# Moving a 256 MB ifftshift through two DMA queues: sixteen-row steps in sequence, against sixteen-row steps sorted into eight classes

## The chip, the cores and the metric

The kernel runs on one core of one Trainium2 chip. The metric is device time in microseconds (us). The core has 16 DMA engines, and every byte of this kernel is moved by them, from DRAM to DRAM; no compute engine touches the data. Both the input and the output hold 8192 x 8192 numbers of 4 bytes, 268.44 MB each.

## The reference

`reference(x)` is `np.fft.ifftshift(x)` on an 8192 x 8192 float32 array. For even sizes that is a swap of diagonal quadrants: `out[r, c] = x[(r + 4096) % 8192, (c + 4096) % 8192]`. No arithmetic is done on the values. Half a row, 4096 numbers or 16 KB, is the longest run that stays contiguous on both sides.

## The kernel before, in words

The output is written as half rows. The left halves (columns 0 to 4095) go through the queue of SyncE (SP, `nc.sync`), the right halves through the queue of ScalarE (ACT, `nc.scalar`). Neither engine does anything but issue DMAs. A helper, `copy` (line 26), works out the source address (line 28) and issues one DMA (line 29) whose source and destination have the same dimensions.

A **step** in this document is 16 neighbouring output rows in one half. It is 16 packets of 16 KB, one for each of the 16 DMA engines: the outermost dimension, `[C, ENGINES]`, has one row for each engine. The rows of a step lie 32 KB apart, so a step spans 512 KB of the array. There are 512 steps in each half; number them from the top of the output, so that step n holds rows 16n to 16n + 15, and consecutive steps lie 512 KB apart. The source of step n is step n + 256 (modulo 512) of the input, in the other half.

A DMA (`back`, line 45) moves 16 steps in falling order: each engine's next packet lies 16 rows, 512 KB, ahead of the last. That is a block of 256 rows and 4096 KB. The loops of lines 47 and 48 go through the 32 blocks from the bottom of the output up, in groups of four. SP takes the blocks of a group in the order 3, 2, 1, 0 (line 49); ACT takes them in the order 1, 0, 3, 2 (line 50). ACT's first block lacks its top step: that step is moved ahead of the loop by seven small DMAs (lines 36 to 42), cut into four strips of 4 KB columns, three of which are cut again by rows (14 + 2, 9 + 7, 4 + 12). So some DMA engines get more small packets than others before the large ones begin, and ACT's sequence has one step less in its first block (`rest`, line 46).

Each DMA gets one of eight completion semaphores in turn. A DMA that takes a semaphore for the second time first waits, on its queue, for the earlier DMA that used it. In the steady part each queue therefore has at most four DMAs in flight.

Of the kernel before, what the change touches and what calls it, by code (L numbers as in the profile page):

```python
# [1 line left out]

# [4 lines left out]


ENGINES = 16


@with_exitstack
def kernel(
    ctx: ExitStack,
    tc: tile.TileContext,
    x: bass.AP,
    out: bass.AP,
):
    nc = tc.nc
    R, C = x.shape  # L20
    hr = R // 2
    hc = C // 2
    per = 16
    rows = ENGINES * per

    def copy(queue, row, col, dims):

        src = (row + hr) % R * C + (col + hc) % C
        queue.dma_start(
            out=bass.AP(out.tensor, out.offset + row * C + col, dims),  # L30
            in_=bass.AP(x.tensor, x.offset + src, dims),
        )

    start = R - 3 * rows
    strip = hc // 4
    for n, k in enumerate((14, 9, 4)):
        col = hc + n * strip
        copy(nc.scalar, start + rows - ENGINES, col, [[C, k], [1, strip]])  # L40
        copy(nc.scalar, start + rows - ENGINES + k, col, [[C, ENGINES - k], [1, strip]])
    copy(nc.scalar, start + rows - ENGINES, hc + 3 * strip, [[C, ENGINES], [1, strip]])


    back = [[C, ENGINES], [-ENGINES * C, per], [1, hc]]
    rest = [[C, ENGINES], [-ENGINES * C, per - 1], [1, hc]]
    for first in range(R - 4 * rows, -1, -4 * rows):
        for n in (3, 2, 1, 0):
            copy(nc.sync, first + n * rows + rows - ENGINES, 0, back)
            right = first + (n + 2) % 4 * rows  # L50
            if right == start:
                copy(nc.scalar, right + rows - 2 * ENGINES, hc, rest)
            else:
                copy(nc.scalar, right + rows - ENGINES, hc, back)


# [1 line left out]
_INS = ['x']  # L58
_OUTS = [((8192, 8192), 'float32')]


# [23 lines left out]
```

## Time and profile before

| what | number |
|---|---|
| time, median of 3 runs | 812.53 us (809.41 to 813.4) |
| profiled execution: span from the first to the last instruction | 810.9 us |
| bytes read and written | 268.44 MB each |
| packets | 17,520, of them 16,368 of 16 KB |
| DMAs issued by SP / ACT | 32 / 39 |

The page of the profile has no work of TensorE, VectorE or ScalarE in it, and 0.2 us of GpSimd. What matters is in its second part (how busy the 16 DMA engines are in 40 slices of the span, and how many GB/s they move), its third part (the two queues: q1 is SP's, q10 is ACT's; their packets and the share of the engines' time that these took) and its sixth (which DMAs were issued, how large). A rate in GB/s counts each byte once, though each is read and written. Besides the page, the trace keeps a record of every packet: its start, its duration, its queue and its size, but not its engine. The profiled span lies inside the range of the three timed runs, 1.6 us under their median, and little lies around it: the first packet starts 2.2 us after the span begins, and the last one ends 1.2 us before it ends.

### The profile page before, as it was taken

The numbers are of one execution on the slowest core, as the hardware profiler recorded it, in microseconds if no ns is written. First come the engines' busy times: TensorE is split into PE (matmuls) and PEld (weight loads), VectorE is DVE, ScalarE is ACT, GpSimd is POOL, SyncE is SP. The second block draws the span as 40 slices with busy tenths as digits, with TensorE's granted clock in tenths as the row PEclk, the third lists the DMA queues.
The fourth block names the chain that finished last, engine by engine and source line by source line (L and its number), as shares of the span: only waits on it lengthen the run. The fifth ranks groups of instructions, "written<-read, shape, count | busy, mean of one in ns | idle before, by whom it ended". The sixth has DMA issues, their size and how long they took to land. (4 is left out here: it accounts for less than half of the span.)

```text
span 810.9 us, 116 instructions
## 1 busy us (share of the span) xinstructions
POOL 0.2 (0%) x4
## 2 busy tenths in 40 slices
POOL 0000000000000000000000000000000000000000
DMA  9999999999999999999999999999999999999998
GB/s 302 328 335 329 334 333 331 331 335 330 326 331 329 331 335 330 332 332 337 335 336 333 333 337 330 334 335 331 336 331 333 335 334 335 333 330 336 333 338 296
DMA packets 17520, 268.44 MB, mean 331 GB/s; under 512 B 1088, under 2 KB 1088, under 8 KB 1152
## 3 DMA queue, kind: packets, MB, share of 16 engines
q1 hardware_dynamic: 8704, 134.22, 49.7%
q10 hardware_dynamic: 8816, 134.22, 49.6%
HBM read 268.44 MB, written 268.44 MB: 662 GB/s over the span
## 5 line engine op out<-in xcount | busy, mean ns | idle before, releaser
L69 POOL MEMSET const-bfloat16-1.0<- 128x1 bf16 x1 | 0.1, 102 | 0.0
L69 POOL MEMSET const-uint8-127<- 128x1 uint8 x1 | 0.1, 102 | 0.0
L69 POOL MEMSET const-float32-0.0<- 128x1 f32 x1 | 0.1, 99 | 0.2 <-issue 0.2
L69 POOL MEMSET const-float32-1.0<- 128x1 f32 x1 | 0.1, 99 | 0.0
## 6 DMA issues: line engine op xcount, KB each, us to landing
out_dram<-in_x_dram SPq DMA_DIRECT2D x32, 4096.0 KB, 100.9
out_dram<-in_x_dram ACTq DMA_DIRECT2D x31, 4096.0 KB
out_dram<-in_x_dram ACTq DMA_DIRECT2D x1, 3840.0 KB
out_dram<-in_x_dram ACTq DMA_DIRECT2D x1, 64.0 KB, 10.8
out_dram<-in_x_dram ACTq DMA_DIRECT2D x1, 56.0 KB
out_dram<-in_x_dram ACTq DMA_DIRECT2D x1, 48.0 KB
out_dram<-in_x_dram ACTq DMA_DIRECT2D x1, 36.0 KB
out_dram<-in_x_dram ACTq DMA_DIRECT2D x1, 28.0 KB
```

The source lines that it names most:

```text
L69: nc = _bacc.Bacc("TRN2", target_bir_lowering=False, num_devices=1)
```

## The change

The steps are sorted into eight **classes**: the class of a step is its number modulo 8, so two steps of one class lie a multiple of 4 MB apart (8 steps of 512 KB). The output is also cut into eight **parts** of 1024 rows (64 steps, 32 MB). A DMA now moves the eight steps of one class in one part, in rising order: each engine's next packet lies 128 rows, 4 MB, further on. That is 2048 KB instead of 4096 KB, so each queue issues 64 DMAs.

The order is set by two loops. `apart` goes from 0 to 7; for each `a` from 0 to 7, `b` is `a ^ apart` (exclusive or). SP moves the left halves of class a in part b, and ACT the right halves of class b in part a. When `apart` is 0 both queues name the same rows; otherwise they name different classes and different parts. Over the loops all 64 pairs of classes occur once. The small strips at the start and the shorter first block of ACT are gone.

```diff
+CLASSES = 8
...
-    per = 16
-    rows = ENGINES * per
+    block = ENGINES * CLASSES
+    steps = R // (block * CLASSES)
 
-    def copy(queue, row, col, dims):
-
+    def copy(queue, cls, part, left):
+        row = part * steps * block + cls * ENGINES
+        col = 0 if left else hc
         src = (row + hr) % R * C + (col + hc) % C
+        dims = [[C, ENGINES], [block * C, steps], [1, hc]]
         queue.dma_start(
...
-    start = R - 3 * rows
-    strip = hc // 4
-    for n, k in enumerate((14, 9, 4)):
-        col = hc + n * strip
-        copy(nc.scalar, start + rows - ENGINES, col, [[C, k], [1, strip]])
-        copy(nc.scalar, start + rows - ENGINES + k, col, [[C, ENGINES - k], [1, strip]])
-    copy(nc.scalar, start + rows - ENGINES, hc + 3 * strip, [[C, ENGINES], [1, strip]])
...
-    back = [[C, ENGINES], [-ENGINES * C, per], [1, hc]]
-    rest = [[C, ENGINES], [-ENGINES * C, per - 1], [1, hc]]
-    for first in range(R - 4 * rows, -1, -4 * rows):
-        for n in (3, 2, 1, 0):
-            copy(nc.sync, first + n * rows + rows - ENGINES, 0, back)
-            right = first + (n + 2) % 4 * rows
-            if right == start:
-                copy(nc.scalar, right + rows - 2 * ENGINES, hc, rest)
-            else:
-                copy(nc.scalar, right + rows - ENGINES, hc, back)
+    for apart in range(CLASSES):
+        for a in range(CLASSES):
+            b = a ^ apart
+            copy(nc.sync, a, b, True)
+            copy(nc.scalar, b, a, False)
```

## The prediction

> **What bounds the kernel now.** I read the second and third part of the page first: how busy the DMA engines are, and with whose packets.
>
> ```profile
> span 810.9 us, 116 instructions
> ...
> DMA  9999999999999999999999999999999999999998
> GB/s 302 328 335 329 334 333 331 331 335 330 326 331 329 331 335 330 332 332 337 335 336 333 333 337 330 334 335 331 336 331 333 335 334 335 333 330 336 333 338 296
> ...
> q1 hardware_dynamic: 8704, 134.22, 49.7%
> q10 hardware_dynamic: 8816, 134.22, 49.6%
> HBM read 268.44 MB, written 268.44 MB: 662 GB/s over the span
> ```
>
> The 16 engines are busy 99.3% of the span (49.7 + 49.6), so nothing waits for an instruction: the end is set by how long packets take. Each engine carries 1,024 packets' worth of 16 KB. The waits of SP's queue confirm that issuing is not the bound:
>
> ```profile
> SPq L29 <- DMA out_dram<-in_x_dram: 686.8, 28, 28.4
> ```
>
> SP stands 686.8 us waiting for an earlier DMA to land before it may issue the next; one issue itself takes 0.57 us in the trace.
>
> So the question is what a packet takes. In the packet records the shortest 16 KB packets take 0.61 us (a third of all, 5,534 of 16,368, lie at or under 0.615), the median 0.73, the mean 0.786, a tenth over 1.07. At 0.611 for all of them the copy would last 1024 x 0.611 = 626 us: some 180 us are packets that are stretched by traffic, and only the addresses and the order of packets can change that. That is what this change does.
>
> **What the trace tells of classes.** An engine's next packet starts 3 to 4 ns before the recorded end of its last one, so the records fall into 16 chains, and counting a queue's packets along a chain gives the step of each. Three readings follow.
>
> (a) All engines keep together: at any time their positions in a queue differ by at most 3 steps, and 93% of an engine's packets alternate between the queues. SP runs 5 to 7 steps ahead of ACT. So the classes of the two queues differ by 1 to 5 at any moment, never by 0.
>
> (b) The class of the step matters. The mean packet of classes 0 to 7 takes 777, 771, 758, 739, 813, 832, 806 and 798 ns. Sorted by the pair (SP's class, ACT's class) the rate of the engines together goes from 320 GB/s for (5, 1) to 358 for (7, 3). But it is no simple function of the difference: mean packets at differences of 1 to 5 are 791, 785, 787, 784 and 790 ns.
>
> (c) Fewer classes in flight cost a little. I take 1 over the sum of squared shares of the classes among the 16 packets in flight as their effective number. It averages 3.5; the mean rate is 333.7. Moments with 4.5 to 5 have 338.5, those under 2.5 (894 moments of 7,474) have 331.5. And while one queue was alone, near the start, all engines were in about 2 classes:
>
> ```profile
> 4.00:23.50 19.50, 0.00 (x0) 1.00 1.00 328
> ```
>
> ```profile
> 18.00:23.50 5.50, 0.00 (x0) 1.00 1.00 319
> ...
> 45.00:805.00 760.00, 0.00 (x0) 1.00 1.00 333
> ```
>
> These are stretches with their GB/s at the end: first nearly all SP and then nearly all ACT, with the strips; then ACT almost alone; then the steady part.
>
> **The change part by part.** I work against the profiled execution: 2.2 us to the first packet, 807.6 us of packets, 1.2 us behind, 810.9 in all.
>
> *Two classes in flight instead of three to five (`apart` 1 to 7, seven eighths of the bytes).* Both queues are issued from 0.73 us on with the same work, so they run within about a step of each other, and a DMA stays in one class for eight steps. The 16 engines are then in class a and class b only. The row for that is reading (c): 331.5 against 333.7. 7/8 x 807.6 = 706.7 us, times 333.7/331.5 - 1 = 0.66%: **+4.7 us**. That all 64 pairs come up adds nothing, since differences of 1 to 5 are alike in (b), and 6 and 7 are 2 and 1 with the queues exchanged. Bounds: if all stages ran like the best pair, 807.6 x 333.7/358 = 753 us, -55; like the worst, 807.6 x 333.7/320 = 842 us, +35.
>
> *One class in flight (`apart` 0, one eighth).* Not in the trace. The nearest row is a queue alone, 319 to 328. I take the slower, 319, since one class is further away than the two there: 100.9 us x (333/319 - 1) = 4.4%: **+4.4 us**. Bounds: the two halves of the same rows, moved one after the other by one engine, could also help; 358 gives -7, and all packets like the class-5 mean (832 against 786 ns) +6.
>
> *Steps 4 MB apart in one queue.* About half of a queue's packets in flight are now one or two steps off in the same class, where before they were one class off. No packets in the trace of before lie so. I take nothing beyond the two terms above, because engines at different steps are in different rows of the 16; below, I take the -55 of the best pair as an end. The upper end is a packet like those over 1 us (2,455 of them, mean 1.155 us): 1024 x 1.155 = 1,183 us. A rule of the Trainium skill speaks against the change here (page "DMA: Bandwidth & Descriptors", section "Latency and other measured facts"): copies between HBM tensors whose rows lie 4 MiB apart ran at 103 GB/s, at 512 KiB apart at 207. An estimate by that page's ratio alone would be 810.9 x 207/103, about 1,630 us. The rule concerns rows moved side by side at that pitch; the trace of before has no such pitch, and side by side the engines stay 32 KB apart here, so no run yet shows it.
>
> *Strips and semaphores.* The seven small DMAs go: 64 packets of 185 ns on 16 engines, **-0.7 us**. DMAs go from 71 to 128, all on 16 engines, so completion packets (4 bytes, 9 ns each) go from 1,088 to 2,048: 960 x 9 / 16 ns = **+0.5 us**.
>
> *Issues.* 57 more, by two queues, at 0.57 to 0.65 us each. They lie beside the packets: when a queue's oldest DMA lands, three more of 8 steps are in flight, 24 packets of an engine at 2 x 0.786 us, 38 us of cover against 0.6 us. Before it was 48 packets. Without this cover each issue would add its 0.6 us plus about 1.4 us to its first packet (the 2.18 us at the start, less the issue's 0.73): 64 x 2 = 128 us. Engines that differ by 3 steps can't use up 24.
>
> *Start and end.* The first 37.8 us after the first packet already run at 334 GB/s, so the simpler start gains nothing. At the end SP's packets stop at 806.0 us and ACT's at 809.7, the 16 engines' last ones within 1.5 us; I count 0, with 1 us to either side. The rising order instead of the falling has no row; 0, inside the bounds of the pairs.
>
> Sum: 4.7 + 4.4 - 0.7 + 0.5 = +8.9 us, 819.8 us on the profiled execution. That one lies 1.6 us under the median of the runs, so **821 us**.
>
> **The rivals.**
>
> *Faster: the new pairs are better ones.* Reading (b) shows pairs from 320 to 358 GB/s, and before covers only 20 of the 64 often. The best six, three with ACT in class 3, one with ACT in class 2 and two with SP in class 3, lie at 340 to 358, in the mean 348.5. If the new pairs are like these, the packets take 807.6 x 333.7/348.5 = 773 us, 777 with start and end. For it: these six lie 2% to 7% over the mean. Against it: in (b) a slow class is slow in either queue (4 to 7 over 0 to 3), and every class has as many packets as before. Half of that gain would be 794.
>
> *No change: only the class's own time counts.* Then the mean of 786 ns stays, whatever the partner, and the single-queue rows are chance (319 is from 5.5 us, some 107 packets). The sum is -0.7 + 0.5: 812 us.
>
> *Much slower: steps of 4 MB collide.* Decides as soon as engines of one queue, a step apart, stand in each other's way. If the 4 packets or so of 16 that are a step off make their kind go at 1.155 us, a quarter of packets is 0.37 us longer, 0.09 us on the mean: 1024 x 0.09 = 94 us, 905 in all; if all do, 1,183. Against it: (a), engines mostly share a step.
>
> *The change doesn't do what it says: the queues drift.* If one gets ahead by 4 steps, half of a DMA's time goes beside the next pair. The classes in flight are then three, and the first term shrinks to some 2 us: 818. That is within the forecast.
>
> **Chances.** What a measurement of this kernel can tell from no change is about 0.5%, 4 us: 808.5 to 816.5 counts as the same. Forecast (two classes in flight, 816.5 to 860): 0.48. Faster pairs, under 808.5: 0.27, of it 0.08 under 785. Same: 0.15. Collisions over 860: 0.10. So faster 0.27, same 0.15, slower 0.58. The range goes from 785 to 860 and leaves out 0.18. The bound of the best pairs (753) and of the collisions (1,183) lie outside it, with those chances; the forecast's own case is 816.5 to 860.
>
> **What would show it.** In the profile after, the 40 slices tell the stages: the first five slices (`apart` 0) should lie at about 319 GB/s and the rest at 330 to 333, with the engines at 99% throughout. If the first eighth is as fast as the rest, the second term is wrong. If all slices lie over 340, the pairs are better ones; if all lie under 310, the 4 MB step costs. Slices in which the engines fall under 95% would mean that queues run dry, which I cost at nothing. A share of packets at 0.61 us that rises with an unchanged mean would say that the stretched ones got longer.

## The result, and the profile after

The changed kernel takes 821.42 us (median of 4 runs, 819.48 to 823.92), the kernel before 811.9 us (809.41 to 813.4) beside it. The ratio is 1.0126, with a 95% interval of 1.0098 to 1.0153: slower, by 9.5 us between the medians. The forecast was 821 us, and its sum +8.9 us.

The page of the changed kernel, second and third part (busy tenths of the DMA engines in 40 slices, GB/s in the same slices, then the queues):

```profile
span 821.9 us, 173 instructions
...
DMA  8999999999999999999999999999999999999998
GB/s 300 329 332 332 322 333 325 332 313 331 320 325 332 329 335 329 319 324 333 335 325 336 325 332 325 325 332 333 329 325 327 335 325 327 337 327 326 325 325 295
...
q10 hardware_dynamic: 9216, 134.22, 49.8%
q1 hardware_dynamic: 9216, 134.22, 49.4%
HBM read 268.44 MB, written 268.44 MB: 653 GB/s over the span
```

The engines are as busy as before (99.2%), so the loss is not idle time; packets take longer. HBM traffic falls from 662 to 653 GB/s. By the packet records the mean 16 KB packet goes from 786.5 to 795.2 ns, and 1,024 packets an engine x 8.7 ns = 8.9 us. The two spans differ by 11.0 us; the rest is gaps between packets (those over 20 ns: 4.6 us an engine before, 6.0 after) and an end in which the engines stop less evenly.

SP's queue by its waits: waiting for, us in total, times, longest.

```profile
SPq L35 <- DMA out_dram<-in_x_dram: 734.5, 60, 15.1
```

60 waits for 64 DMAs, 734.5 us: SP is still always ahead of the packets. Stretches of the changed kernel (start and end, length, POOL, clock, DMA share, GB/s):

```profile
2.20:103.00 100.80, 0.00 (x0) 1.00 1.00 330
103.00:820.00 717.00, 0.00 (x0) 1.00 1.00 328
```

The first line is the stage in which `apart` is 0, the second the seven others. The first was forecast as the slow one. It is not.

### The profile page after: what moved, and what is told of

It is laid out like the page before. It is cut to its first block, busy times and chain, and to the rows that moved or that the text cites. A ratio compares the mean times of both kernels' runs of the same rounds, so it can differ in the third digit from the quotient of the medians.

```text
span 821.9 us, 173 instructions
## 1 busy us (share of the span) xinstructions
POOL 0.2 (0%) x4
## 2 busy tenths in 40 slices
DMA packets 18432, 268.44 MB, mean 327 GB/s; under 512 B 2048, under 2 KB 2048, under 8 KB 2048
```

## The experiments

Every kernel was timed beside the kernel before on the same chip, and its ratio is to that. This matters: the kernel before took 811.34 us beside the first four kernels below and 810.97 beside the next four, but 821.47 and 822.1 us on the two chips of the last four. So only ratios are compared across chips, not times. The changed kernel itself was not timed again beside them: its 1.0126 comes from the result above, where the kernel before took 811.9 us, and its ratio on the two slower chips is not known.

Theory A: a step is one class, and when the steps of a queue that are in flight together are all of one class, packets stretch each other. Theory B: the rising order costs. Theory C: the frame costs (2 MB DMAs, no strips, which queue is ahead).

**Neighbouring steps in the changed frame**

```diff
-        row = part * steps * block + cls * ENGINES
+        apart_by = 1 * ENGINES
+        row = part * steps * block + cls // 1 * steps * apart_by + cls % 1 * ENGINES
...
-        dims = [[C, ENGINES], [block * C, steps], [1, hc]]
+        dims = [[C, ENGINES], [apart_by * C, steps], [1, hc]]
```

> The changed kernel's loops, DMA size and rising order, but the eight steps of a DMA are neighbours (512 KB apart, all eight classes). Theory A, one class in flight per queue is the cost: about 812 us, like the kernel before. Theory B, the rising order is the cost: about 821. Theory C, the frame (2 MB DMAs, no strips, ACT ahead of SP) is the cost: about 821.

Measured: 812.06 us, ratio 1.0005 (0.9985 to 1.0025). Only the distance between the eight steps of a DMA was put back, and the whole loss is gone. The frame costs nothing that shows: C falls.

**Steps 2 MB apart** (the same edit with 4 for 1; two classes in turn)

> As the changed kernel, but the eight steps of a DMA lie 2 MB apart: two classes in turn instead of one. Theory A: between the two kernels, 815 to 819 us. Theories B and C: about 821. If the distance of 4 MB itself collides, a clear drop below 817.

Measured: 819.39 us, ratio 1.0092 (1.0068 to 1.0115), just over what theory A gave. Most of the loss is there already with two classes: by the interval between half of it and nearly all, and the middle is close to the kernel in falling order below.

**Falling order**

```diff
-        row = part * steps * block + cls * ENGINES
+        row = (part + 1) * steps * block - block + cls * ENGINES
...
-        dims = [[C, ENGINES], [block * C, steps], [1, hc]]
+        dims = [[C, ENGINES], [-block * C, steps], [1, hc]]
```

> The changed kernel with the eight steps of each DMA in falling order. Theory A: about 821 us, as in rising order. Theory B: nearly all of the loss goes, about 812 to 814. Theory C: about 821.

Measured: 820.38 us, ratio 1.0103 (1.008 to 1.0126). B falls from this side.

**The kernel before, rising**

```diff
-    start = R - 3 * rows
+    start = 2 * rows
...
-    back = [[C, ENGINES], [-ENGINES * C, per], [1, hc]]
+    forth = [[C, ENGINES], [ENGINES * C, per], [1, hc]]
...
-    for first in range(R - 4 * rows, -1, -4 * rows):
-        for n in (3, 2, 1, 0):
-            copy(nc.sync, first + n * rows + rows - ENGINES, 0, back)
+    for first in range(0, R, 4 * rows):
+        for n in (0, 1, 2, 3):
+            copy(nc.sync, first + n * rows, 0, forth)
```

> The kernel before mirrored: the same strips, blocks of 16 neighbouring steps, but blocks and steps in rising order. Theory A: about 812 us. Theory B: about 821. Theory C: about 812.

Measured: 810.93 us, ratio 0.9992 (0.9977 to 1.0007). B falls from the other side too.

The steady parts show the same as the times: first the changed kernel, then neighbouring steps, 2 MB, 4 MB falling, and the kernel before rising (last column GB/s).

```profile
45.00:800.00 755.00, 0.00 (x0) 1.00 1.00 328
```

```profile
45.00:800.00 755.00, 0.00 (x0) 1.00 1.00 334
```

```profile
45.00:800.00 755.00, 0.00 (x0) 1.00 1.00 331
```

```profile
45.00:800.00 755.00, 0.00 (x0) 1.00 1.00 329
```

```profile
45.00:800.00 755.00, 0.00 (x0) 1.00 1.00 334
```

So the distance counts. Is it the distance as such, or the class that 4 MB keeps?

**16 MB apart, one class**, and **16.5 MB apart, all classes**

```diff
-        row = part * steps * block + cls * ENGINES
+        row = (part // 4 * 256 + part % 4 * 8 + cls) * ENGINES
...
-        dims = [[C, ENGINES], [block * C, steps], [1, hc]]
+        dims = [[C, ENGINES], [32 * ENGINES * C, steps], [1, hc]]
```

> The changed kernel's loops with the eight steps of a DMA 32 steps (16 MB) apart, so still in one class. Theory A1, what counts is that a queue's neighbouring steps are in one class: about 820 us, as with 4 MB. Theory A2, what counts is how far an engine's next packet lies: 820 or more, perhaps slower still.

Measured: ratio 1.0115 (1.0093 to 1.0137). The second kernel turns 32 into 33 steps:

```diff
+        off = part % 4 * 8 + cls
+        full = min(steps, 32 - off)
+        for at, n in ((off, full), (off + 33 * full - 32, steps - full)):
...
+            row = (part // 4 * 256 + at) * ENGINES
+            dims = [[C, ENGINES], [33 * ENGINES * C, n], [1, hc]]
```

> As the last, but 33 steps (16.5 MB) apart, so that the eight steps of a DMA go through all eight classes; where they would leave the half of the array, a DMA is cut in two, 78 DMAs a queue for 64. Theory A1: about 812 us, as with neighbouring steps. Theory A2: about 820, as with one class.

Measured: ratio 1.0022 (1.0007 to 1.0038), with 28 DMAs more in all, on the same chip. Its steady part, behind that of the kernel with 32 steps:

```profile
45.00:800.00 755.00, 0.00 (x0) 1.00 1.00 330
```

```profile
45.00:800.00 755.00, 0.00 (x0) 1.00 1.00 333
```

One step more of distance takes away four fifths of the loss (1.15% to 0.22%). At nearly the same distance the class decides. The 0.22% that is left is not explained: the 28 more DMAs, some of them short, and the distance both remain possible.

How many classes there are is not settled. No step of 1 MB was run, and the interval of the 2 MB kernel overlaps those of the kernels with 4 and 16 MB. Sorted modulo 2 MB instead of 4 MB, into four classes, the packets in flight set the two groups apart as well. Their effective number, taken as in reading (c) of the prediction with the steps counted from the 4-byte packet that ends each DMA on each engine, is 1.5 to 1.7 in the four kernels above with a loss of about 1% (the changed one among them 1.5, 2 MB 1.6) and 1.8 to 2.1 in the kernel before, its mirror, and those of neighbouring steps and 16.5 MB. So the runs show a cost of steps of 2, 4 and 16 MB, not that 4 MB is the period.

**Reads alone, writes alone** (both put the rows elsewhere than the reference; `near` is the row of neighbouring steps)

```diff
+        near = part * steps * block + cls * steps * ENGINES
+        near_dims = [[C, ENGINES], [ENGINES * C, steps], [1, hc]]
...
-            out=bass.AP(out.tensor, out.offset + row * C + col, dims),
+            out=bass.AP(out.tensor, out.offset + near * C + col, near_dims),
```

> Leaves the reference: the source goes in steps 4 MB apart as in the changed kernel, the destination in neighbouring steps, so the rows land elsewhere. Theory A with reads as the cost: about 820 us. With writes as the cost: about 812. With both needed or both sharing: 812 to 818.

Measured: ratio 1.0046 (1.0028 to 1.0065). The other kernel gives `near` to the source and leaves the destination in one class:

> Leaves the reference: the destination goes in steps 4 MB apart, the source in neighbouring steps. Theory A with writes as the cost: about 820 us. With reads as the cost: about 812. With both sharing: 814 to 818.

Measured: ratio 1.0089 (1.0067 to 1.0111). Both sides cost, writes about twice as much (the two intervals just miss each other); 0.46 + 0.89 = 1.35% lies near the whole (1.26%). In these two a packet's read and write are also no longer in one class, which was not separated.

**Both queues in one class all the time**

```diff
-            copy(nc.scalar, b, a, False)
+            copy(nc.scalar, a, b, False)
```

> The changed kernel with ACT taking the right halves of the very rows whose left halves SP takes, all the time: both queues in one class, as in the changed kernel's first eighth. The prediction's second term (one class in flight runs like a queue alone, 319 against 333 GB/s): 7/8 of 807.6 us x 4.4% more than the sum of the first term, about 845 us. The rival, only the neighbours within a queue count and the other queue's class does not: 818 to 821 us.

Measured: ratio 1.0162 (1.0146 to 1.0178). Neither theory's number: beside the changed kernel's 1.0126 (and 1.0103, 1.0115 of its like) the other queue's class costs 0.4 to 0.6%, not 4.4%. That difference is taken across chips. On its own chip the steady part of this kernel, the first line, can be set beside that of a kernel below with all classes in flight at once and a ratio of 1.0, the second:

```profile
45.00:800.00 755.00, 0.00 (x0) 1.00 1.00 324
```

```profile
45.00:800.00 755.00, 0.00 (x0) 1.00 1.00 329
```

**A queue alone** (the kernel with neighbouring steps, and `nc.sync` for both copies)

> Neighbouring steps (512 KB apart), all 128 DMAs issued by SP, none by ACT: a queue alone for the whole time. If the rows of a queue alone near the start of the kernel before (319 to 328 GB/s) were a price of standing alone: 824 to 847 us. If they were chance: about 812.

Measured: ratio 1.0064 (1.0043 to 1.0085). Its page has all packets on q1:

```profile
span 824.0 us, 173 instructions
...
q1 hardware_dynamic: 18432, 268.44, 99.1%
```

A queue alone costs 0.6% with neighbouring steps, far less than the 4.4% that the row of 319 GB/s gave, and more than nothing. Fewer classes in flight are not the reason: counted from the packets that end the DMAs, the effective number is 2.8 here and 2.7 in the kernel before. The reason stays open.

**All classes in flight at once**

```diff
-        row = part * steps * block + cls * ENGINES
+        row = (part * CLASSES + cls) * block
...
-        dims = [[C, ENGINES], [block * C, steps], [1, hc]]
+        dims = [[steps * C, ENGINES], [C, steps], [1, hc]]
```

> Same DMA size and loops, but each DMA covers 128 neighbouring rows with engine n on rows 8n to 8n + 7, so the 16 engines stand 256 KB apart, two in each of all eight classes, and an engine's next packet lies in the next row. Theory A1 carried on (about 2% of rate from 1.7 to 3.8 classes in flight): faster than before, 800 to 808 us. Rival, only that a queue's classes turn over counts, and more at once gain nothing: about 812. Rival, the 16 neighbouring rows of a step help each other: slower, over 818.

Measured: ratio 1.0 (0.9988 to 1.0011). The gain of a theory A carried on does not come: beyond the three to five classes of the kernel before, more are worth nothing. No version here is faster than the kernel before by more than its interval.

**All classes at once, but 4 MB from an engine's packet to its next**

```diff
-        row = part * steps * block + cls * ENGINES
+        row = part * steps * block + cls
...
-        dims = [[C, ENGINES], [block * C, steps], [1, hc]]
+        dims = [[CLASSES * C, ENGINES], [block * C, steps], [1, hc]]
```

> Each step has its 16 rows 8 rows (256 KB) apart, so the engines stand in all eight classes at once, while each engine's next packet in the queue lies 4 MB on, in the class of its last. Read as a ratio to the kernel before on the same chip. Theory A1, the classes in flight at one time count: 1.000, as with neighbouring steps. Theory D, an engine's packet collides with its own last one 4 MB away (its write still on the way): 1.010 to 1.013, as in the changed kernel.

Measured: ratio 1.002 (1.0009 to 1.003). Each engine stays in one class for eight packets, as in the changed kernel, yet the loss is 0.2% and not 1.0 to 1.3%, with the other engines in other classes. So it is mostly packets of different engines that stretch each other; an engine's own last packet has at most 0.3% of it, the end of the interval. This holds if the changed kernel loses as much on this chip, where no kernel with one class was run.

## Why the prediction was right, step by step

**What bounds the kernel.** Right. The engines are busy 99.2% after the change, and longer packets are 8.9 of the 11.0 us between the spans. The sum had nothing for the gaps between packets, which grew by 1.4 us an engine.

**First term, two classes in flight (+4.7 us).** The mechanism is right and is shown: one class or two per queue cost (1.0092 to 1.0126), eight in turn cost little or nothing (0.9992 to 1.0022), at the distances and in the orders tried. The term was mis-sized. By the records the seven stages with `apart` 1 to 7 have a mean packet of 795.5 ns; 896 packets x 9.0 ns = 8.1 us.

The row that priced it, reading (c), was weak, and that it came within a factor of two is luck. It sets 894 moments of the kernel before beside the mean, 2.2 GB/s apart, where the rate from moment to moment scatters by 31 GB/s. The steps can be counted more firmly from the 4-byte packet that ends each DMA on each engine: the 16 engines end one DMA within 1.7 us (SP's) and 2.3 us (ACT's) in the mean, not much over the 1.6 us that a step takes. Counted so, the kernel before has 2.7 effective classes, not 3.5, and its moments under 2.5 lie 0.2 GB/s under the mean, with a standard error of 0.6: the effect is not seen inside it. It is seen between the kernels, with 2.5 classes and 335.6 GB/s for neighbouring steps, 2.2 and 333.1 for 2 MB, 1.6 and 329.7 in the changed kernel; and inside the kernel with neighbouring steps, where moments under 2.0 lie 8.8 GB/s under the mean, with a standard error of 1.2. Why the kernel before does not show it is open.

**Second term, one class in flight (+4.4 us).** This step failed. "The nearest row is a queue alone" took 5.5 us of a start for a price. That row is 107 packets with a mean of 818 ns and a standard error of 21, less than two standard errors over the 786 of all packets. The stage has a mean packet of 792.6 ns (standard error 4.0), 128 x 6.1 ns = 0.8 us against before and no more than the other stages; with both queues in one class throughout, the extra is 0.4 to 0.6%, some 0.5 us on an eighth. The kernel that uses one queue shows that the row was chance or mixed in something else: standing alone costs 0.6%, and the wider window with 328 GB/s, 1.5% under the steady part, was the better estimate. The sum came out because one term was too small by 3.4 us and the other too large by 3.6. That is luck; the sign and the rough size rest on the first term alone.

**Steps 4 MB apart in one queue (nothing beyond the two terms, an end at 1,183 us).** Right that nothing collides beyond the class effect: 4 MB and 16 MB cost the same (1.0126 and 1.0115), and 16.5 MB nearly nothing (1.0022). The rule of the Trainium skill (page "DMA: Bandwidth & Descriptors", section "Latency and other measured facts") that rows 4 MiB apart halve the rate points the right way and is far too strong here: 1.0126 was measured. The rule's own case, rows side by side at that pitch, was not run: in the changed kernel the 16 rows of a step lie 32 KB apart. In the order of pitches (512 KiB good, 2 MiB worse, 4 MiB worst) the ratios of these runs agree with it, 1.0005, 1.0092 and 1.0126, though the intervals of the last two overlap.

**Strips, semaphores, issues, order (-0.7, +0.5, 0, 0).** Right together, as far as the intervals tell: the changed frame with neighbouring steps stands at 1.0005, the kernel before in rising order at 0.9992, and falling order at 1.0103 beside the 1.0126 of rising. The cover held: SP waits 734.5 us.

**Queues within a step of each other.** Wrong. SP's first packet starts 5.0 us into the span, ACT's at 2.2, and ACT stays two to four steps ahead. So at the edge of a DMA three classes can be in flight; what that is worth was not separated, and over the whole the effective number is still under two.

**The rivals.** No change and collisions are excluded by 1.0098 to 1.0153. The premise of better pairs falls: the classes' own times are no property of the class. Counted from the packets that end the DMAs, classes 0 to 3 are the fast ones in the kernel before (765 ns in the mean, against 808 for 4 to 7), and 4 to 7 in the changed kernel (783 against 807). In the changed frame with neighbouring steps it is 4 to 7 too (738 against 824), so it is not the 4 MB; in the kernel before in rising order it is 0 to 3 (773 against 793), so it is not the direction. What sets it is open; the rates of 20 pairs in one kernel were no basis for another.

## What to carry to other kernels

When every engine is busy all the time, ask which addresses are in flight together: read the packet records for the lengths, and name the rows that neighbouring packets of all engines touch. In these runs steps of 2, 4 and 16 MB between the packets of a queue cost about 1%, and one block of 16 rows more, 16.5 MB for 16, took most of the loss away. And price a stage that the trace doesn't hold from a long stretch or not at all: a start of 5 us is a mean of a hundred packets, here with a standard error of 2.5%, and can have other things in it.

## What the runs showed of the hardware

Queues whose neighbouring steps lie a multiple of 4 MB apart cost 1.0 to 1.3% of the time, and 2 MB apart 0.9%; whether the period is 4 MB or less is not shown. Writes alone cost 0.89% and reads alone 0.46%. The three to five classes in flight of the kernel before are enough: eight at once give no more (ratio 1.0). The direction of the addresses costs nothing that shows (0.9992), nor does the frame as a whole, DMAs of 2 MB for 4 MB without the strips (1.0005). One queue for all packets costs 0.6%. One and the same kernel took 811 us on some chips and 821 to 822 us on others, about as much as the change itself.
